# A hybrid encoder layer: rotation tables kept as halves, weight casts issued inside the gates' products, three pairs open at the start of the second SwiGLU

## The chip, the cores and the metric

One core of one Trainium2 chip runs the whole layer. The metric is the device time of one execution in microseconds (us). TensorE multiplies, VectorE (DVE), ScalarE (ACT) and GpSimd (POOL) do the rest; SyncE (SP) and ScalarE issue most of the DMAs.

## The reference

```python
# x: (1, 1024, 1024) float32; D_MODEL 1024, D_FF 2816
h = x + 1/2 * SwiGLU(RMSNorm(x))                  # SwiGLU(x) = (silu(x @ Wg) * (x @ Wu)) @ Wd
z = RMSNorm(h) @ W_in                             # 512 ssm | 512 q | 512 k | 512 v | 1024 gate | 1024 gate
A = GLU(bidirectional S5 of z.ssm) -> 1024        # 32 groups of 16 channels, 64 complex states each
B = 2-D neighbourhood attention of q, k, v -> 1024
h = h + (sigmoid(gate_ssm) * A + sigmoid(gate_att) * B) @ W_out
h = h + 1/2 * SwiGLU(RMSNorm(h))
out = RMSNorm(h)
```

S5 is the linear recurrence s[t] = lambda s[t-1] + B u[t] with complex diagonal lambda, over 1024 positions in both directions, and y[t] = Re(C s[t]).

## The kernel before

**Products.** Everything lies transposed in SBUF, 128 features by two halves of 512 positions. A float32 operand is split in two parts that TensorE takes: hi, a cast by ScalarE, and lo, the rest, a subtraction by VectorE. A product is three: hi x hi, hi x lo, lo x hi. All of them are issued through `mm` (L265), so line 265 stands for nearly all matmuls.

**Weights.** The class `Weights` holds one list of units in the order in which TensorE will need them. A unit "u" is a weight of 128 x 1024 (cast L191, subtraction L192); a unit "p" is one of seven 128 x 512 blocks of a gate and up pair (L176, L202); a unit "h" is a half of a down weight. Raw weights come by SyncE's queue into five buffers `wr` and are issued as buffers come free; split ones lie in eight buffers `wp`. `next(ahead)` prepares units up to `ahead` beyond the current one and hands out the current one. `fill` prepares more while there is room, and may make the cast of the next unit without its subtraction (`cast_one`); `self.cast` and `self.split` count the units whose cast and whose subtraction have been issued. Raw buffers come free when a unit is split, so `drop` and `load` follow it.

**The SwiGLUs.** After some plain blocks in the first layer, a gate and up pair is computed in seven products instead of eight, on sums of blocks (Strassen's way, in Winograd's form): the weights' sums S by VectorE (L134, four a pair, issued by `early` and `step`), the activations' T1 to T4 by VectorE, too. `FIRST` writes out by hand in which order the first pairs' products come: entry "61" is product 6 of the second pair. Before, the first layer has 21 entries with three pairs open at a time, the second 28 with four. Products 1 and 2 need only blocks of the activations themselves; products 6, 7, 5 and 4 need T2, T3, T1 and T4, product 3 the last block scaled. `feed` calls the steps that form the T after given numbers of products; `T` can only be scaled when the normalisation (`rstd`, then a spread product with `diag`) is there. Near the end of a layer, `feed` also loads and splits the first operands of the down projection (`down_load`, `down_split`).

**S5 among the gates.** The state space part is cut in 16 blocks b of two groups. `ssm_steps` is a generator of 21 rounds of seven steps; one step is taken every seven matmuls of the products that run then, so that a round n works on several blocks: enter (block n-4: L265 ps<-su,let, evacuated by ScalarE as ev, L1066 and L1067), rotation (L1079, L1080), leave (block n-5: ps<-sx,lo), scan (L1094) and a second rotation, the shift into sx by ScalarE (L1106, L1107) with the operands of block n-2 (four transposes L1028), the table (block n-3), the powers (L993). The rotation multiplies by a table of cosines and sines over 128 positions: `ssm_table` makes it every fourth round for four blocks, by seven doublings of three instructions each (L1002), each doubling the length by the angle sum rule; the last is made in two parts.

The gates are 16 products of 48 matmuls (`gates`, the units are "u"), whose results ScalarE evacuates and stores (L1229, L1230). With `W.next()`, product c prepares unit c+2 at its start: cast by ScalarE, then subtraction by VectorE, each in its engine's order of issue among the scan's steps.

**Merge and project.** `merge` forms m = sigmoid(gate_ssm) A + sigmoid(gate_att) B for eight blocks d and two halves: x times the first product, y times the second, the sum by GpSimd, and the split of the half before (`ended`). `project` multiplies m by W_out, half 0 first, and adds to h; `done` accumulates the squares for the next normalisation. During half 1, `early(3)` issues three sums of the coming pairs behind d = 4, 5 and 6.

Of the kernel before, what the change touches and what calls it, by code (L numbers as in the profile page):

```python
# [15 lines left out]
P = 128  # L16
KD = 8
# [21 lines left out]
def hs(half):  # L39
# [7 lines left out]
FILLED, ACT, TAIL = 7, 24, 3  # L47
NP = NF // 2

FIRST = (  # L50
    "10 11 12 20 21 22 60 61 70 71 50 51 40 41 62 30 31 72 52 42 32",
    "10 11 12 20 21 22 13 60 61 23 70 71 50 51 40 41 62 30 31 72 52 42 32 63 73 53 43 33",
)
THEN = (1, 6, 2, 7, 5, 4, 3)


def order_of(fs):

    first = [(int(x[1]), int(x[0])) for x in FIRST[len(fs) == NF].split()]
    return [(fs[i], q) for i, q in first] + [(f, q) for f in fs[max(i for i, _ in first) + 1 :] for q in THEN]  # L60


class Weights:
# [85 lines left out]
    def step(self, n=1):  # L149
        for _ in range(min(n, len(self.steps))):  # L150
            self.steps.pop(0)()

    def cast_one(self):

        u = self.units[self.cast]
        if u[0] == "h":
            i = u[1]
            self.load(i + 1)
            src = self.tiles[i][:, :HALF]
        else:  # L160
            p, q = u[1:]
            if q < 3:
                i = self.pairs[p]["raw"]
                self.load(i + 1)
                while i not in self.tiles:
                    self.step()
                    self.load(i + 1)
                src = self.tiles[i][:, hs(q - 1)]
            else:
                self.blocks(p)  # L170
                src = self.pairs[p]["S"][q]
                if q == 6:
                    self.step(5)
        t = self.pool.tile([P, 1024], F32R, tag="wp", name="wp", bufs=PARTS)
        hi, lo = t[:, :HALF], t[:, HALF:]
        self.nc.scalar.copy(hi, src)  # L176
        self.casts[self.cast] = (hi, lo, src)
        self.cast += 1

    def prepare_one(self):  # L180
        nc, u = self.nc, self.units[self.split]
        if u[0] == "u":
            i = u[1]
            self.load(i + 1)
            raw = self.tiles[i]
            n = self.raws[i].shape[1]
            hi, lo = (self.pool.tile([P, 1024], F32R, tag="wp", name="wp", bufs=PARTS) for _ in (0, 1))

            cuts = [0, P, n] if self.split < 2 else [0, n]
            for a, b in zip(cuts, cuts[1:]):  # L190
                nc.scalar.copy(hi[:, a:b], raw[:, a:b])  # L191
                nc.vector.tensor_tensor(  # L192
                    out=lo[:, a:b], in0=raw[:, a:b], in1=hi[:, a:b].bitcast(F32), op=ALU.subtract
                )
            self.parts[self.split] = (hi, lo)
            self.drop(i)
            self.cast += 1
        else:
            if self.cast == self.split:
                self.cast_one()  # L200
            hi, lo, src = self.casts.pop(self.split)
            nc.vector.tensor_tensor(out=lo, in0=src, in1=hi.bitcast(F32), op=ALU.subtract)  # L202
            self.parts[self.split] = (hi, lo)
            if u[0] == "h":
                self.drop(u[1])
            else:
                self.done(*u[1:])
        if self.split in self.jobs:
            self.job(*self.jobs.pop(self.split))
        self.split += 1  # L210
        self.load(len(self.raws))

        if u[0] == "p":
            for v in self.units[self.split : self.split + 4]:
                if v[0] == "p" and v[2] > 2 and self.loaded >= self.pairs[v[1]]["raw"] + 2:
                    self.blocks(v[1])
# [43 lines left out]
class Body:  # L260
# [362 lines left out]
    def feed(self, steps, plain, others={}):  # L623
        rest = {4: ("T3",), 5: ("b12",), 6: ("t1",), 7: ("T1",), 8: ("b22",), 9: ("t4",), 10: ("T4",), 12: ("B22",)}
        last = 7 * (NF - plain) - 1

        def after(n):
            for x in rest.get(n, ()):
                steps[x]()
            if n in others:  # L630
                others[n]()

            if n == last - 5:
                for i in range(2):
                    self.down_load(i)
            if n == last - 1:
                self.down_split(0)

        self.early = ({}, {})
        self.gate_up(plain, after)  # L640
# [357 lines left out]

    def ssm_table(self, b):

        nc, pool, st = self.nc, self.ssm, self.ss[b]
        m = lambda o, x, y, op: nc.vector.tensor_tensor(out=o, in0=x, in1=y, op=op)  # L1002
        if b % 4 == 0:
            tab = self.tab = pool.tile([P, 2, 8, P], F32, tag="tab", name="tab", bufs=1)
            nc.vector.memset(tab[:, 0, :, 0], 1.0)
            nc.vector.memset(tab[:, 1, :, 0], 0.0)
            for i in range(7):
                n = 1 << i

                for a, k in ((0, 8),) if i < 6 else ((0, 4), (4, 4)):  # L1010
                    gs = slice(2 * b + a, 2 * b + a + k)
                    sh = [P, 2, k, n]
                    old, new = tab[:, :, a : a + k, 0:n], tab[:, :, a : a + k, n : 2 * n]
                    y = pool.tile([P, 512], F32, tag="ty", name="ty", bufs=1)[:, : 2 * k * n]
                    y = y.rearrange("p (c g j) -> p c g j", c=2, g=k)
                    m(new, old, self.cosines[:, i, gs].unsqueeze(1).unsqueeze(3).to_broadcast(sh), ALU.mult)
                    m(y, old[:, ::-1], self.sines[:, i, :, gs].unsqueeze(3).to_broadcast(sh), ALU.mult)
                    m(new, new, y, ALU.add)
        st["tab"] = (self.tab, slice(2 * (b % 4), 2 * (b % 4) + 2))

    def ssm_operands(self, b):

# [47 lines left out]
    def rotate(self, x, st):  # L1070

        nc, pool = self.nc, self.ssm
        tab, gs = st["tab"]
        c = tab[:, 0, gs, :].rearrange("p g j -> p (g j)")
        s = tab[:, 1, gs, :].rearrange("p g j -> p (g j)")
        ta = pool.tile([P, 2, 2 * P], F32, tag="ta", name="ta", bufs=1)
        tb = pool.tile([P, 2, 2 * P], F32, tag="tb", name="tb", bufs=1)
        xx = x.rearrange("p c g j -> p c (g j)")
        nc.vector.tensor_tensor(out=ta, in0=xx, in1=c.unsqueeze(1).to_broadcast([P, 2, 2 * P]), op=ALU.mult)  # L1079
        nc.vector.tensor_tensor(out=tb, in0=xx, in1=s.unsqueeze(1).to_broadcast([P, 2, 2 * P]), op=ALU.mult)  # L1080
        return ta, tb
# [138 lines left out]
    def gates(self, u):  # L1220

        nc, W = self.nc, self.W
        for c in range(16):
            w = W.next()
            banks = [self.bank(), self.bank()]
            yield from self.passes(banks, w, lambda i: slice(i * P, i * P + P), *u, range(KD))
            for half in (0, 1):
                g = self.big.tile([P, HALF], F32, tag="b", name="g")
                nc.scalar.copy(g, banks[half])  # L1229
                nc.scalar.dma_start(out=self.gs[c, :, hs(half)], in_=g)  # L1230
# [310 lines left out]
    def merge(self, s, a):  # L1541
# [42 lines left out]
        for d in range(KD):  # L1584
            w = ahead.pop(0) if ahead else W.next()
            pool, tag, n = (self.big, "b", None) if d < 4 else (self.tmp, "act", ACT)
            hi, lo = ([pool.tile([P, HALF], F32R, tag=tag, name="m", bufs=n) for _ in (0, 1)] for _ in (0, 1))
            for half in (0, 1):
                x, y = g.pop((d, 0, half)), g.pop((d, 1, half))
                ps = bs.pop((d, half)) if d < 2 else product(s, w, 0, half)  # L1590
                nc.vector.tensor_tensor(out=x, in0=x, in1=ps, op=ALU.mult)
                ps = product(a, w, 4, half, (3,), ba.pop((d, half))) if d < 2 else product(a, w, 4, half)
                nc.vector.tensor_tensor(out=y, in0=y, in1=ps, op=ALU.mult)
                nc.gpsimd.tensor_tensor(out=x, in0=x, in1=y, op=ALU.add)
                while ended:
                    self.split(*ended.pop(0))
                ended.append((hi[half], lo[half], x))
                if d and ready:
                    scaled(ready[0])
                    sigmoid(ready.pop(0))  # L1600
                if d and (d, half) > (1, 0):
                    load()
            mh.append(hi)
            ml.append(lo)
# [3 lines left out]
    def project(self, m, h, done):  # L1608
        nc, W = self.nc, self.W
        for half in (0, 1):  # L1610
            for d in range(KD):
# [3 lines left out]
                self.poke()  # L1615
                nc.vector.tensor_tensor(out=h[d][half], in0=h[d][half], in1=ps[half], op=ALU.add)
                done(d, half)
                if half and 3 < d < KD - 1:
                    W.early(3)
                if half and d == KD - 2:  # L1620
                    W.fill(PARTS - 2)


    def build(self):
# [303 lines left out]
```

## Time and profile before

| | |
|---|---|
| three runs | 2101.65, 2102.79, 2104.61 us; median 2102.79 |
| the profiled execution | 2104.78 us, its span 2103.0 us |
| TensorE busy (PE) | 2010.0 us, 96% |
| weight loads (PEld) | 1640.2 us, 78% |
| VectorE (DVE) | 1436.6 us, 68% |
| ScalarE (ACT) | 843.9 us, 40% |
| GpSimd (POOL) | 163.5 us, 8% |
| DMA | 315.55 MB, mean 150 GB/s |
| TensorE's granted clock, mean | 0.982 |

The span runs from the first to the last instruction; the shares are of it. The granted clock is a share of 2.4 GHz. PE's busy time contains the time that matmuls take longer at a lower clock. In a row of a timeline, [6.09 <-ACT wp L191] says that the engine was idle for 6.09 us before it, and what released it.

### The profile page before, as it was taken

The numbers are of one execution on the slowest core, as the hardware profiler recorded it, in microseconds if no ns is written. First come the engines' busy times: TensorE is split into PE (matmuls) and PEld (weight loads), VectorE is DVE, ScalarE is ACT, GpSimd is POOL, SyncE is SP. The second block draws the span as 40 slices with busy tenths as digits, with TensorE's granted clock in tenths as the row PEclk, the third lists the DMA queues.
The fourth block names the chain that finished last, engine by engine and source line by source line (L and its number), as shares of the span: only waits on it lengthen the run. The fifth ranks groups of instructions, "written<-read, shape, count | busy, mean of one in ns | idle before, by whom it ended". The sixth has DMA issues, their size and how long they took to land.

```text
span 2103.0 us, 26597 instructions
## 1 busy us (share of the span) xinstructions
PE 2010.0 (96%) x9394; PEld 1640.2 (78%) x9394; DVE 1436.6 (68%) x2655; ACT 843.9 (40%) x1548; POOL 163.5 (8%) x192
## 2 busy tenths in 40 slices
PE   8999999999999998897999999998899999999997
PEld 6878888878888887676877778776688888878886
DVE  6986666658676667856475778667866666657556
ACT  7333223324645233333354573334323332334454
POOL 0001111000000111110000303101001100000000
PEclk9999999999999999998999999999999999999998
DMA  4447666647665332222421333535366565457563
GB/s 182 115 148 178 180 186 175 155 157 271 219 203 192 96 104 81 85 85 82 141 83 49 98 114 132 201 114 129 112 172 181 149 189 155 136 184 270 175 206 117
DMA packets 160358, 315.55 MB, mean 150 GB/s; under 512 B 20352, under 2 KB 31776, under 8 KB 160224
## 3 DMA queue, kind: packets, MB, share of 16 engines
q1 hardware_dynamic: 133920, 274.79, 38.9%
q0 software_dynamic: 15232, 27.59, 8.2%
q10 hardware_dynamic: 11072, 11.47, 1.6%
q8 instruction: 74, 1.21, 0.2%
q14 instruction: 60, 0.49, 0.1%
HBM read 243.83 MB, written 116.10 MB: 171 GB/s over the span
## 4 chain that ended last, share of the span: by engine, by line
PE 68%; DVE 19%; ACT 6%; DMA 3%; issue 2%; ACTq 1%; SPq 0%; POOL 0%; DVEq 0%; POOLq 0%
PE ps L265 67%; DVE wp L192 1%; DVE tab L1002 1%; DVE tq L352 1%; ACT wp L191 1%; DVE gl L1559 1%; DVE wp L202 1%; DMA wr<-in_wu 1%; DVE ta L1079 1%; DVE le L993 1%; DVE ww L1094 1%; DVE lo L993 1%; DVE lt L993 1%; DVE tb L1080 1%; DMA y<-ys 1%
## 5 line engine op out<-in xcount | busy, mean ns | idle before, releaser
L265 PE MATMUL ps<-tq,wp 128*128 128x512 f32 x3444 | 793.2, 392 | 16.5 <-DVE u L576 4.7
L265 PEld LDWEIGHTS ps<-tq,wp 128*128 128x128 f32 x3444 | 651.1, 189 | 157.8 <-ACT t L597 4.4
L265 PE MATMUL ps<-ap,wp 128*128 128x512 f32 (+1 forms) x1884 | 428.9, 389 | 7.4 <-ACT ap L351 4.5
L265 PEld LDWEIGHTS ps<-ap,wp 128*128 128x128 f32 x1884 | 351.6, 190 | 83.2 <-ACT ap L351 5.7
L265 PE MATMUL ps<-uh,wp 128*128 128x512 f32 x1088 | 326.2, 405 | 8.7 <-ACT wp L191 8.7
L265 PEld LDWEIGHTS ps<-uh,wp 128*128 128x128 f32 x1088 | 205.0, 193 | 58.5 <-ACT wp L191 10.1
L202 DVE TENSOR_TENSOR wp<-wr,wp 128x512 fp32r<-128x512 f32 x318 | 217.4, 686 | 34.7 <-ACT wp L176 34.7
L176 ACT CAST wp<-wr 128x512 fp32r<-128x512 f32 x318 | 194.3, 614 | 62.8 <-PE ps L265 49.8
L265 PE MATMUL ps<-ul,wp 128*128 128x512 f32 x544 | 183.8, 400 | 0.7 <-DVE ul L331 0.7
L192 DVE TENSOR_TENSOR wp<-wr,wp 128x1024 fp32r<-128x1024 f32 (+2 forms) x72 | 85.5, 1191 | 121.6 <-ACT wp L191 121.3
L351 ACT CAST ap<-ar 128x512 fp32r<-128x512 f32 x154 | 95.4, 619 | 116.9 <-DMA ar<-tq 106.7
L352 DVE TENSOR_TENSOR ap<-ar,ap 128x512 fp32r<-128x512 f32 x154 | 105.8, 687 | 47.5 <-ACT ap L351 47.3
L265 PEld LDWEIGHTS ps<-ul,wp 128*128 128x128 f32 x544 | 102.9, 192 | 21.8 <-DVE ul L331 1.1
L176 ACT CAST wp<-ws 128x512 fp32r<-128x512 f32 x123 | 75.5, 618 | 101.5 <-PE ps L265 72.3
L606 ACT ACTIVATE v<-v 128x512 f32<-128x512 f32 x41 | 25.9, 632 | 221.9 <-DVE v L576 210.9
L265 PE MATMUL ps<-m,wp 128*128 128x512 f32 x384 | 90.6, 396 | 5.2 <-ACT m L351 3.3
L265 PEld LDWEIGHTS ps<-m,wp 128*128 128x128 f32 x384 | 73.0, 191 | 22.0 <-ACT m L351 3.7
L202 DVE TENSOR_TENSOR wp<-ws,wp 128x512 fp32r<-128x512 f32 x123 | 84.1, 685 | 0.0
L688 DVE SCALAR_TENSOR_TENSOR h<-ps,h 128x512 f32<-128x512 f32 (+1 forms) x76 | 48.6, 657 | 51.6 <-PE ps L265 51.6
L96 POOL DMA_DIRECT2D sums<-in_wd x44 | 37.3, 948 | 590.9 <-DMA sums<-in_wd 590.8
L576 DVE TENSOR_TENSOR v<-t,ps 128x512 f32<-128x512 f32 x41 | 28.1, 686 | 70.8 <-PE ps L265 70.8
L191 ACT CAST wp<-wr 128x1024 fp32r<-128x1024 f32 (+2 forms) x72 | 71.0, 995 | 10.0 <-ACT g L1229 7.2
(208 smaller groups left out, 2184.8 us busy)
## 6 DMA issues: line engine op xcount, KB each, us to landing
ar<-tq SPq DMA_DIRECT2D x154, 256.0 KB
wr<-in_wg SPq DMA_DIRECT2D x44, 512.0 KB
wr<-in_wu SPq DMA_DIRECT2D x44, 512.0 KB
sums<-in_wd SPq DMA_DIRECT2D x88, 256.0 KB
wr<-sums SPq DMA_DIRECT2D x88, 256.0 KB
wr<-in_wd SPq DMA_DIRECT2D x66, 256.0 KB
tq<-t SPq DMA_DIRECT2D x61, 256.0 KB
wr<-in_w_in SPq DMA_DIRECT2D x28, 512.0 KB
```

The lines of the kernel that those rows point to most:

```text
L96: self.nc.gpsimd.dma_start(out=out, in_=x, accum_op=ALU.add, max_dma_last_dim=2048)
L176: self.nc.scalar.copy(hi, src)
L191: nc.scalar.copy(hi[:, a:b], raw[:, a:b])
L192: nc.vector.tensor_tensor(out=lo[:, a:b], in0=raw[:, a:b], in1=hi[:, a:b].bitcast(F32), op=ALU.subtract)
L202: nc.vector.tensor_tensor(out=lo, in0=src, in1=hi.bitcast(F32), op=ALU.subtract)
L265: self.nc.tensor.matmul(out, lhsT, rhs, start=start, stop=stop, skip_group_check=go_on)
L351: self.nc.scalar.copy(hi, x)
L352: self.nc.vector.tensor_tensor(out=lo, in0=x, in1=hi.bitcast(F32), op=ALU.subtract)
L576: add = lambda o, u, v: nc.vector.tensor_tensor(out=o, in0=u, in1=v, op=ALU.add)
L606: nc.scalar.activation(out=s["v"], in_=s["v"], func=AF.Silu, scale=-1.0)
L688: nc.vector.scalar_tensor_tensor(out=t, in0=bank[:, sl], scalar=c, in1=t, op0=ALU.mult, op1=ALU.add)
L993: m = lambda o, x, y, op: self.nc.vector.tensor_tensor(out=o, in0=x, in1=y, op=op)
```

## The change

- **Tables in halves.** The table of four blocks holds 64 positions instead of 128, after six doublings. For each block a tile `own` of 128 positions is filled: two ScalarE copies of the first 64, and one doubling of three VectorE instructions into the last 64. `rotate` reads `own`.
- **Casts in the gates' products.** After matmul 24 of each gates' product, `cast_ahead` issues ScalarE's cast of the next unit, if no unit is cast but not split; `prepare_one` then only subtracts.
- **Second layer's order.** Both layers use the order of 21 entries, with three pairs open.
- **Sums among more projections.** `early(4)` behind d = 3, 4 and 5 in the place of `early(3)` behind 4, 5 and 6, and the `fill` behind d = 6 is gone.
- **Merge and down operands.** The split of the half before is issued ahead of the second product's multiplication; the very last sum is VectorE's. The first operands of the down projection are loaded and the first is split two products earlier.

```diff
-FIRST = ("10 11 12 20 21 22 60 61 70 71 50 51 40 41 62 30 31 72 52 42 32",
-    "10 11 12 20 21 22 13 60 61 23 70 71 50 51 40 41 62 30 31 72 52 42 32 63 73 53 43 33",)
+FIRST = "10 11 12 20 21 22 60 61 70 71 50 51 40 41 62 30 31 72 52 42 32"
...
+    def cast_ahead(self):
+        if self.cast == self.split and self.units[self.cast][0] == "u":
+            i = self.units[self.cast][1]
+            if i < self.loaded:
+                hi, lo = (self.pool.tile([P, 1024], F32R, tag="wp", name="wp", bufs=PARTS) for _ in (0, 1))
+                n = self.raws[i].shape[1]
+                self.nc.scalar.copy(hi[:, :n], self.tiles[i][:, :n])
+                self.casts[self.cast] = (hi, lo)
+                self.cast += 1
...
-            if n == last - 5:
+            if n == last - 7:
                 for i in range(2):
                     self.down_load(i)
-            if n == last - 1:
+            if n == last - 3:
                 self.down_split(0)
...
+        def double(new, old, i, a, k):
+            ...
+            m(new, old, self.cosines[:, i, gs].unsqueeze(1).unsqueeze(3).to_broadcast(sh), ALU.mult)
+            m(y, old[:, ::-1], self.sines[:, i, :, gs].unsqueeze(3).to_broadcast(sh), ALU.mult)
+            m(new, new, y, ALU.add)
...
-            tab = self.tab = pool.tile([P, 2, 8, P], F32, tag="tab", name="tab", bufs=1)
+            tab = self.tab = pool.tile([P, 2, 8, 64], F32, tag="tab", name="tab", bufs=1)
...
-            for i in range(7):
+            for i in range(6):
...
+        own = pool.tile([P, 2, 2, P], F32, tag="own", name="own", bufs=2)
+        old = self.tab[:, :, 2 * (b % 4) : 2 * (b % 4) + 2, :]
+        for c in (0, 1):
+            nc.scalar.copy(own[:, c, :, 0:64], old[:, c])
+        double(own[:, :, :, 64:P], old, 6, 2 * b, 2)
+        st["tab"] = own
...
-            yield from self.passes(banks, w, lambda i: slice(i * P, i * P + P), *u, range(KD))
+            for n, _ in enumerate(self.passes(banks, w, lambda i: slice(i * P, i * P + P), *u, range(KD))):
+                if n == 24:
+                    W.cast_ahead()
+                yield
...
+                while ended:
+                    self.split(*ended.pop(0))
                 ps = product(a, w, 4, half, (3,), ba.pop((d, half))) if d < 2 else product(a, w, 4, half)
                 nc.vector.tensor_tensor(out=y, in0=y, in1=ps, op=ALU.mult)
-                nc.gpsimd.tensor_tensor(out=x, in0=x, in1=y, op=ALU.add)
-                while ended:
-                    self.split(*ended.pop(0))
+                (nc.vector if (d, half) == (KD - 1, 1) else nc.gpsimd).tensor_tensor(out=x, in0=x, in1=y, op=ALU.add)
...
-                if half and 3 < d < KD - 1:
-                    W.early(3)
-                if half and d == KD - 2:
-                    W.fill(PARTS - 2)
+                if half and 2 < d < 6:
+                    W.early(4)
```

## Rows read from the trace of the kernel before

**Rows 1.** Windows: stretch, length, busy PE, PEld, DVE, ACT, POOL; granted clock; DMA share; GB/s.

```profile
740.00:1000.00 260.00, 229.48 (x1172) 191.25 (x1171) 179.68 (x366) 87.43 (x165) 27.73 (x47) 0.94 0.27 86
800.00:820.00 20.00, 16.73 (x81) 14.05 (x81) 19.14 (x40) 4.96 (x10) 3.27 (x6) 0.92 0.29 85
820.00:840.00 20.00, 18.85 (x89) 15.93 (x90) 10.41 (x19) 8.03 (x15) 1.78 (x3) 0.83 0.27 87
880.00:900.00 20.00, 14.59 (x65) 12.32 (x64) 13.60 (x24) 5.05 (x9) 1.78 (x3) 0.83 0.21 68
960.00:980.00 20.00, 8.63 (x37) 7.23 (x36) 13.57 (x27) 5.71 (x10) 1.78 (x3) 0.66 0.19 63
819.80:893.10 73.30, 64.65 (x328) 53.53 (x328) 52.58 (x110) 25.07 (x50) 8.79 (x15) 0.95 0.27 86
1405.00:1515.00 110.00, 94.54 (x383) 74.60 (x382) 90.85 (x151) 45.12 (x77) 6.69 (x8) 0.94 0.44 127
```

**Rows 2.** TensorE's waits, 700 to 1020 us: total, times, longest.

```profile
PE ps L265 <- ACT sx L1107: 26.2, 9, 11.4
```

**Rows 3.** Timeline of VectorE, a plain round: start, length, instruction, idle before.

```profile
835.84 0.76 DVE L1103 TENSOR_TENSOR ta<-ta,tb 128x256 f32<-128x256 f32 x2
...
842.70 1.22 DVE L192 TENSOR_TENSOR wp<-wr,wp 128x1024 fp32r<-128x1024 f32 x1 [6.09 <-ACT wp L191]
...
847.89 0.69 DVE L1079 TENSOR_TENSOR ta<-ev,tab 128x512 f32<-128x512 f32 x1
...
852.62 0.76 DVE L1103 TENSOR_TENSOR ta<-ta,tb 128x256 f32<-128x256 f32 x2
```

**Rows 4.** Timeline of ScalarE, the same round.

```profile
836.63 0.62 ACT L1106 COPY sx<-ta 64x508 f32<-64x508 f32 x1 [9.29 <-DVE ta L1103]
...
841.61 1.05 ACT L191 CAST wp<-wr 128x1024 fp32r<-128x1024 f32 x1 [0.41 <-ACT g L1229]
...
843.15 0.58 ACT L1067 COPY ev<-ps 64x512 f32<-64x512 f32 x1
```

**Rows 5.** Timeline of TensorE, another plain round.

```profile
916.03 0.60 PE L1028 MATMUL ps<-ident,le 128*128 128x128 f32 x4
...
922.46 1.05 PE L265 MATMUL ps<-su,let 128*128 128x128 f32 x8
...
928.05 0.71 PE L265 MATMUL ps<-sx,lo 128*128 128x128 f32 x4 [1.13 <-ACT sx L1107]
...
932.49 0.60 PE L1028 MATMUL ps<-ident,le 128*128 128x128 f32 x4
```

**Rows 6.** Timeline of VectorE, a round that makes a table.

```profile
872.60 0.07 DVE L1005 MEMSET tab<- 128x8 f32 x1
...
875.65 0.42 DVE L1002 TENSOR_TENSOR ty<-tab,sines 128x256 f32<-128x256 f32 x1
...
878.62 0.69 DVE L1002 TENSOR_TENSOR tab<-tab,kept 128x512 f32<-128x512 f32 x1
```

**Rows 7.** Timelines of TensorE and VectorE, opening of the second layer.

```profile
1408.28 16.61 PE L265 MATMUL ps<-m,wp 128*128 128x512 f32 x72 [1.60 <-ACT wp L191]
...
1415.58 0.68 DVE L134 TENSOR_TENSOR ws<-wr 128x512 f32<-128x512 f32 x1
...
1438.56 1.02 PE L265 MATMUL ps<-diag,ones 128*128 128x512 f32 x2
...
1445.83 0.68 DVE L431 TENSOR_TENSOR tf<-tf,ps 128x512 f32<-128x512 f32 x1
```

**Rows 8.** Chain of the work that ended last, same opening: start, length, what.

```profile
1412.97 3.91 DMA wr<-in_wg
...
1437.84 6.10 DMA wr<-in_wu
```

**Rows 9.** Timeline of TensorE, end of the merge.

```profile
1334.79 0.51 PE L265 MATMUL ps<-m,wp 128*128 128x512 f32 x1 [3.25 <-ACT m L351]
```

**Rows 10.** Timeline of TensorE, beginning of the first down projection.

```profile
461.47 0.50 PE L265 MATMUL ps<-ap,wp 128*128 128x512 f32 x1 [2.31 <-ACT ap L351]
```

More of the change, by code (lines that the diff above doesn't have):

```diff
@@ L48 @@
 NP = NF // 2
[L50 to L53, printed above, removed]
+FIRST = "10 11 12 20 21 22 60 61 70 71 50 51 40 41 62 30 31 72 52 42 32"
 THEN = (1, 6, 2, 7, 5, 4, 3)
 def order_of(fs):
-    first = [(int(x[1]), int(x[0])) for x in FIRST[len(fs) == NF].split()]
+    first = [(int(x[1]), int(x[0])) for x in FIRST.split()]
     return [(fs[i], q) for i, q in first] + [(f, q) for f in fs[max(i for i, _ in first) + 1 :] for q in THEN]
@@ L186, in prepare_one @@
             n = self.raws[i].shape[1]
-            hi, lo = (self.pool.tile([P, 1024], F32R, tag="wp", name="wp", bufs=PARTS) for _ in (0, 1))
+            if self.split in self.casts:
+                hi, lo = self.casts.pop(self.split)
+            else:
+                hi, lo = (self.pool.tile([P, 1024], F32R, tag="wp", name="wp", bufs=PARTS) for _ in (0, 1))
             cuts = [0, P, n] if self.split < 2 else [0, n]
             for a, b in zip(cuts, cuts[1:]):
-                nc.scalar.copy(hi[:, a:b], raw[:, a:b])
+                if self.cast == self.split:
+                    nc.scalar.copy(hi[:, a:b], raw[:, a:b])
                 nc.vector.tensor_tensor(
@@ L196, in prepare_one @@
             self.drop(i)
-            self.cast += 1
+            self.cast = self.split + 1
         else:
@@ L1002, in ssm_table @@
         m = lambda o, x, y, op: nc.vector.tensor_tensor(out=o, in0=x, in1=y, op=op)
+        def double(new, old, i, a, k):
+            n = old.shape[-1]
+            gs = slice(a, a + k)
+            sh = [P, 2, k, n]
+            y = pool.tile([P, 512], F32, tag="ty", name="ty", bufs=1)[:, : 2 * k * n]
+            y = y.rearrange("p (c g j) -> p c g j", c=2, g=k)
+            m(new, old, self.cosines[:, i, gs].unsqueeze(1).unsqueeze(3).to_broadcast(sh), ALU.mult)
+            m(y, old[:, ::-1], self.sines[:, i, :, gs].unsqueeze(3).to_broadcast(sh), ALU.mult)
+            m(new, new, y, ALU.add)
         if b % 4 == 0:
-            tab = self.tab = pool.tile([P, 2, 8, P], F32, tag="tab", name="tab", bufs=1)
+            tab = self.tab = pool.tile([P, 2, 8, 64], F32, tag="tab", name="tab", bufs=1)
             nc.vector.memset(tab[:, 0, :, 0], 1.0)
             nc.vector.memset(tab[:, 1, :, 0], 0.0)
-            for i in range(7):
+            for i in range(6):
                 n = 1 << i
[L1010 to L1019, printed above, removed]
+                double(tab[:, :, :, n : 2 * n], tab[:, :, :, 0:n], i, 2 * b, 8)
+        own = pool.tile([P, 2, 2, P], F32, tag="own", name="own", bufs=2)
[4 more added lines that the diff above has]
+        st["tab"] = own
     def ssm_operands(self, b):
@@ L1072, in rotate @@
         nc, pool = self.nc, self.ssm
-        tab, gs = st["tab"]
-        c = tab[:, 0, gs, :].rearrange("p g j -> p (g j)")
-        s = tab[:, 1, gs, :].rearrange("p g j -> p (g j)")
+        tab = st["tab"]
+        c = tab[:, 0].rearrange("p g j -> p (g j)")
+        s = tab[:, 1].rearrange("p g j -> p (g j)")
         ta = pool.tile([P, 2, 2 * P], F32, tag="ta", name="ta", bufs=1)
```

## The prediction

> **What bounds the kernel now.** I read the page first, then the windows, then TensorE's waits by stretch, then one round of the stretch that lost most. TensorE is busy for 96% of the span, so no change can bring more than the few per cent in which it stands or runs at half clock. The windows say where these are: from 740 to 1000 us it is busy for 229.48 of 260 us, 30.5 idle, and in four 20 us windows of that stretch its granted clock is 0.92, 0.83, 0.83 and 0.66 [rows 1]. The clock has two levels, 1.2 and 2.4 GHz, so a busy microsecond at a mean of 0.83 does 0.83 us of work: 16.73 x 0.08 + 18.85 x 0.17 + 14.59 x 0.17 + 8.63 x 0.34 = 9.9 us. The stretch loses 40.4 us in all. The other large loser is 1405 to 1515 us, the opening of the second SwiGLU: 15.5 idle and 94.54 x 0.06 = 5.7 by the clock, 21 us [rows 1].
>
> In the first stretch the gates' projections run and the S5 scan is threaded through them. Almost all of TensorE's idle time there ends with ScalarE's sx [rows 2]. A plain round is a ring of two engines. VectorE ends the scan (L1103, 835.84), then stands 6.09 us until ScalarE has cast the next weight (842.70), splits it, does the powers, rotates (847.89), scans, and ends the next scan: 852.62 - 835.84 = 16.78 us [rows 3]. ScalarE stands 9.29 us for VectorE, copies sx, evacuates, and reaches the cast only at 841.61 [rows 4]. Neither is full; each waits for the other. TensorE has less to do: from one round's transposes to the next 932.49 - 916.03 = 16.46 us, of which 1.13 is the wait for sx, so 15.33 us of work [rows 5].
>
> **The early cast.** It is the edit that counts. The cast of a later weight moves from the end of a product to its middle, after 24 of 48 matmuls. In ScalarE's queue it then stands behind ev and ahead of sx of the same round, inside the 9.29 us in which ScalarE does nothing [rows 4]. Its buffers are those of the product before, which TensorE has ended, and its raw weight was issued several products earlier, so it adds no wait. VectorE goes from L1103 straight on. Its next possible wait is ev: from sx to the end of ev it was 843.73 - 836.63 = 7.1 us, less the cast's 0.95, plus half a microsecond for the new copies, 6.7 us; then rotation and scan, 853.4 - 847.9 = 5.5. That ring is 12.2 us, under TensorE's 15.33, so TensorE sets the pace.
>
> **Tables in halves.** Of a table the memsets and six doublings stay: 878.62 - 872.60 = 6.0 us [rows 6]. The seventh goes: six instructions of 0.69, 4.1 us. Each of the four blocks gets three instructions of 256 elements at 0.42 [rows 6], 1.26 us a round, and two ScalarE copies a quarter the size of ev's, which take 1.2 the pair [rows 4]: 0.5, at most 1.2. VectorE does 0.9 us more in four rounds, but no longer ten in a piece. Is there room? Four rounds took 73.30 us, with VectorE busy 52.58 and some 2 in gaps between its own instructions (a plain round's own work is 16.78 - 6.09 = 10.69) [rows 1, 3]. With the halves that is 55.5; TensorE needs 4 x 15.33 and half a microsecond for a small product, 61.8.
>
> The lag of a table round is covered too. After its enter (922.46) TensorE asks for sx of the round before at 926.92, 4.5 us on [rows 5], so sx of this round is due 15.33 + 4.5 = 19.8 us after this enter. The scan ends 7.6 us after it (0.9 enter, 1.2 ev, 5.5). In a table round VectorE then waits for the small product, about 1.5 us behind the transposes, which come 10.0 after enter: 11.5. Then 0.3, the table's 6.0, 1.26, split and powers 5.2, the next scan 5.5 and sx 1.3: 31.1. It is due at 15.33 + 19.8 = 35.1. Four microseconds are spare, and each plain round behind it gives 3 more. So I count all stalls of the stretch as gone, and with them the low clock, which the windows show only where TensorE had waited.
>
> An instruction of 256 elements takes 0.42 us and one of 512 takes 0.69, so half the width does not take half the time [rows 6]. The Trainium skill, "VectorE: DVE Perf Modes", section "The TRN2 errata", speaks against this edit: instructions on SBUF pay a fixed latency each, and it advises tiles of at least 512 elements. The trace agrees on the price, 12 x 0.42 - 6 x 0.69 = 0.9 us per four rounds. By the rule, were VectorE the pace, four tables would give back 3.6 us and the time would be 2068; by the rows it is not the pace, and I cost it at nothing.
>
> Sum of the stretch: 40.4 by windows. By rounds: 73.3 - 61.8 = 11.5 for four, 2.9 for each of the 13 between the first table and the last long wait, 37. I take 38. Bounds 30 and 40.4.
>
> **The merge.** TensorE waits 3.25 us for m at its end [rows 9]. That is the cast of the half before the last, which in ScalarE's queue still stands behind the same sigmoid, which waits for VectorE's scaling. Splitting before the second product moves one VectorE instruction of 0.6. The last sum on VectorE instead of GpSimd concerns a half that the projection reads eight products later. I take 0; bounds -0.6 and +0.6.
>
> **The second layer's opening.** Three effects. (a) The fourth pair's first product needed a raw weight issued at 1437.84 that took 6.10 us; ScalarE's cast waited for it, and VectorE behind the cast, so that the scaling of T began at 1445.83 [rows 7, 8]. The seventh product of the new order reads sums formed long before, so VectorE can scale T when the spread product is there, 1438.56 + 1.02 = 1439.6: 6.2 us won on the engine that is dense from there on. (b) Two products that need no T are gone from ahead of it, so each set of operands is due 24 x 16.61 / 72 = 5.5 us sooner [rows 7]; 5.5 lost. Three pairs fit the banks, so waits for a bank turn into waits for T4 and for evacuations. (c) The first pair's four sums now stand ahead of the split that frees a buffer for the second pair's gate weight. A sum's row shows 0.68 us; neighbours overlap, so I count 0.6 each, 2.4 in all. That weight's issue moves from 1412.97 to 1415.4, and it lands 3.91 us later, or 6.10, the two transfers that the chain shows [rows 8], at 1419.3 or 1421.5. VectorE reaches the sums that read it 2.4 after 1415.6 [rows 7], at 1418.0, and stands 1.3 to 3.5 us. Three sums, 1.8 us, leave the place between the last two projections; there VectorE waits for products anyway, so little of it comes back. Counted to the last row sum, on which the normalisation waits, I take 1.1 us lost, 3.2 at worst. Together -6.2 + 5.5 + 1.1 = +0.4, which I take as 0. Bounds -6 and +8.7, and up to 5 more by the clock.
>
> **Down projections.** The first operand is split two products earlier: about 0.2 us of waiting goes in each layer. The large wait there, 2.31 us [rows 10], is for an operand that is still issued behind the first product. -0.5 in all; bounds -1 and +0.5.
>
> **Sum.** The profiled execution took 2104.8 us, 1.8 of it outside the span of 2103.0. 2104.8 - 38 - 0.5 = 2066.3. It lies 2.0 over the median of the runs, 2102.8, so I forecast **2064**.
>
> **Rivals.**
> (A) The copies become the new wait. ScalarE writes one half of own and VectorE the other. If they are ordered by tile and not by region, VectorE stands in every round until ScalarE is through sx, two evacuations and the copies, some 3.5 of the 4.98 us from sx to the cast [rows 4]. VectorE's plain round is then 10.69 + 1.26 + 3.5 = 15.4, TensorE's pace with nothing left for the tables, so four rounds take about 61.8 + 6. Gain 37 - 13 x 1.5 = 18: 2084. For it: sx stands ahead of the copies. Against: no such wait between two writers of one buffer is in the waits, though no row excludes it either. 11%.
> (B) VectorE, full to 90%, still comes late in the table rounds. Of waits of up to 11.4 us [rows 2] some 2.5 stay in each of four, 10 us with the clock. 2074. 8%.
> (C) The early cast does nothing, as it is made only where two counters agree: the ring of 16.78 stays, the copies put 0.5 ahead of the cast in each round, the shorter table gives 4 back in four. 2103. 2%.
> (D) Slower: the opening of the second layer. Place: the first products on T1 and T4, with VectorE dense (90.85 of 110 [rows 1]). Price: 8.7 and 5 by the clock, 14. It decides only if the gates bring less than 14: with 7 there, 2110; with nothing, 2117. 5%, as the ring would have to hold too.
>
> **How the numbers follow.** Forecast 74%, with a range of its own of 2058 to 2071 (gates 33 to 40.4, opening -3 to +3). The range, 2056 to 2086, takes in B, A and most of the opening's -6. A measurement of this kernel tells about 0.2%, 4 us, from no change. Faster 74 + 11 + 8 = 93%, within 0.2% 2%, slower 5%.
>
> **What would show it.** Right: in the gates' stretch TensorE waits for sx no more than 1 us in sum, its clock reads 1.00, a round takes 15.3 to 15.6 us, and the cast lies ahead of sx. VectorE waiting for own's copies would mean A; waits for sx behind the four tables alone, B; VectorE still waiting 6 us for the cast, C. In the opening no wait of 10 us of ScalarE for a weight, and a new wait of TensorE of 4 to 6 us ahead of T4's first product; if it runs through there, my 5.5 was too high. I am wrong as a whole if the gates' stretch is not at least 30 us shorter.

## The result, and the profile after

The changed kernel takes 2064.35 us (median of four runs, 2062.95 to 2069.7) against 2103.39 (four runs): a ratio of 0.9814, with a 95% interval of 0.98 to 0.9828. The profiled execution took 2063.81 us, its span 2062.0, 41.0 us less than before; between the two medians it is 39.0. The forecast of 2064 was met, but that it was met so closely is luck: its sum held two misses that nearly cancel.

Landmarks on TensorE cut both executions at the same work: the first table product (ps<-cs,flat), the first product of the values (ps<-wp,uh), the first and the last of the projection (ps<-m,wp), and the first and the last of the second layer's down projection (ps<-ap,wp). Each length below is the difference of two starts or ends in the timeline.

| stretch, us | before | after | difference | in the forecast |
|---|---|---|---|---|
| up to the table product (first layer, four projections) | 701.05 | 700.01 | -1.0 | -0.5 for the two down projections together |
| gates with the scan | 292.67 | 249.87 | -42.8 | -38 |
| values, attention, first part of the merge | 334.48 | 334.44 | 0 | 0 |
| projection, with the wait for the merge's end | 96.69 | 102.41 | +5.7 | 0 |
| second SwiGLU with its opening | 442.77 | 441.90 | -0.9 | 0 |
| its down projection | 223.66 | 221.17 | -2.5 | in the -0.5 above |

The gates first. The windows of the changed kernel, columns as in [rows 1]: the first is the stretch of [rows 1], the second holds the same 1331 matmuls that before took 262.28 us of TensorE's busy time in a stretch of 292.80.

```profile
740.00:1000.00 260.00, 260.00 (x1369) 218.85 (x1369) 198.46 (x412) 110.35 (x215) 32.40 (x51) 1.00 0.33 109
700.00:950.00 250.00, 250.00 (x1331) 209.78 (x1330) 209.47 (x442) 102.98 (x213) 34.94 (x59) 1.00 0.34 108
```

TensorE never stands there, and its clock stays at 2.4 GHz. VectorE's timeline shows the rounds behind a table, to be held against [rows 3]:

```profile
852.81 0.42 DVE L1015 TENSOR_TENSOR own<-tab,kept 128x256 f32<-128x256 f32 x1
...
863.86 0.76 DVE L1123 TENSOR_TENSOR ta<-ta,tb 128x256 f32<-128x256 f32 x2
864.54 1.22 DVE L204 TENSOR_TENSOR wp<-wr,wp 128x1024 fp32r<-128x1024 f32 x1
...
871.25 0.69 DVE L1099 TENSOR_TENSOR ta<-ev,own 128x512 f32<-128x512 f32 x1 [0.50 <-ACT ev L1087]
...
875.98 0.76 DVE L1123 TENSOR_TENSOR ta<-ta,tb 128x256 f32<-128x256 f32 x2
...
898.49 0.69 DVE L1099 TENSOR_TENSOR ta<-ev,own 128x512 f32<-128x512 f32 x1 [3.42 <-ACT ev L1087]
```

The subtraction (L204) now follows the end of the scan at once. From one end of a scan to the next, 863.86 to 875.98, it is 12.1 us, against 16.78 before; after two such rounds VectorE has caught up and waits 3.42 us for ev, that is, for TensorE. ScalarE, to be held against [rows 4], makes the cast (L157) behind ev and 5.5 us ahead of sx:

```profile
882.83 0.58 ACT L1087 COPY ev<-ps 64x512 f32<-64x512 f32 x1
883.44 1.05 ACT L157 CAST wp<-wr 128x1024 fp32r<-128x1024 f32 x1
...
888.98 0.62 ACT L1126 COPY sx<-ta 64x508 f32<-64x508 f32 x1 [1.83 <-DVE ta L1123]
```

TensorE's pace is the distance of two enters, 15.02 us:

```profile
866.13 1.05 PE L277 MATMUL ps<-su,let 128*128 128x128 f32 x8
...
881.15 1.05 PE L277 MATMUL ps<-su,let 128*128 128x128 f32 x8
```

The merge is the loss. TensorE's waits of the changed kernel from 1280 to 1460 us (total, times, longest): the first row answers to [rows 9], the last lies between the projection's halves and is 1.60 us as before [rows 7], the others belong to the second layer's opening.

```profile
PE ps L277 <- ACT m L363: 8.7, 1, 8.7
PE ps L277 <- ACT tq L363: 5.4, 1, 5.4
PE ps L277 <- DVE acc L296: 3.8, 1, 3.8
PE ps L277 <- DVE u L588: 2.9, 1, 2.9
PE ps L277 <- ACT wp L203: 1.6, 1, 1.6
```

And the opening on TensorE and VectorE, answering to [rows 7]: VectorE waits for the spread product (3.02 us) and scales T 1.06 us after that product's start, where it was 7.27 before; T4's first product then waits 5.37 us.

```profile
1403.21 1.02 PE L277 MATMUL ps<-diag,ones 128*128 128x512 f32 x2
...
1404.27 0.69 DVE L443 TENSOR_TENSOR tf<-tf,ps 128x512 f32<-128x512 f32 x1 [3.02 <-PE ps L277]
...
1438.85 3.65 PE L277 MATMUL ps<-tq,wp 128*128 128x512 f32 x7 [5.37 <-ACT tq L363]
```

### The profile page after: what moved, and what is told of

It is laid out like the page before. It is cut to its first block, busy times and chain, and to the rows that moved or that the text cites. A ratio compares the mean times of both kernels' runs of the same rounds, so it can differ in the third digit from the quotient of the medians.

```text
span 2062.0 us, 26647 instructions
## 1 busy us (share of the span) xinstructions
PE 1994.0 (97%) x9394; PEld 1629.6 (79%) x9394; DVE 1435.7 (70%) x2680; ACT 852.5 (41%) x1580; POOL 162.0 (8%) x191
## 4 chain that ended last, share of the span: by engine, by line
PE 83%; DVE 9%; ACT 3%; DMA 3%; issue 1%; SPq 0%; POOL 0%; ACTq 0%; DVEq 0%
PE ps L277 82%; DMA y<-ys 1%; DVE tq L364 1%; DVE wp L214 1%; PE ps L1369 1%; DMA h<-in_x 1%; DVE wp L204 1%; DMA wr<-in_wg 1%; DVE ws L131 0%; DMA ar<-tq 0%; ACT sq L294 0%; DVE h L432 0%; PE ps L1048 0%; DVE tf L443 0%; DVE gl L1582 0%
## 5 line engine op out<-in xcount | busy, mean ns | idle before, releaser
L204 DVE TENSOR_TENSOR wp<-wr,wp 128x1024 fp32r<-128x1024 f32 (+2 forms) x72 | 84.6, 1179 | 52.1 <-ACT wp L203 51.9
L609 ACT COPY t<-ps 128x512 f32<-128x512 f32 x41 | 24.0, 586 | 112.9 <-PE ps L277 112.9
```

Of the source, the lines that this page charges most:

```text
L204: nc.vector.tensor_tensor(out=lo[:, a:b], in0=raw[:, a:b], in1=hi[:, a:b].bitcast(F32), op=ALU.subtract)
L609: nc.scalar.copy(s["t"], ps)
```

## The experiments

Two groups of four, each group on one chip. The ratios are to runs of the kernel before on the same chip. The lengths are those of the landmarks, from one profiled execution each: gates / projection with the wait for the merge's end / second SwiGLU / its down projection. Of old merge this execution is the shortest of its four (2054.49 us, the median is 2060.06), of old opening the longest of its five (2070.91, the median is 2067.83).

| kernel | gates | projection | second SwiGLU | down | time, ratio to before |
|---|---|---|---|---|---|
| before | 292.67 | 96.69 | 442.77 | 223.66 | |
| after | 249.87 | 102.41 | 441.90 | 221.17 | 0.9814 (0.98 to 0.9828) |
| cast alone | 251.29 | 96.68 | 443.41 | 222.75 | 0.9804 (0.979 to 0.9818) |
| halves alone | 291.71 | 96.71 | 442.78 | 223.48 | 1.0001 (0.9992 to 1.001) |
| old merge | 249.87 | 96.72 | 439.79 | 220.64 | 0.9775 (0.9759 to 0.9792) |
| old opening | 249.87 | 102.57 | 442.96 | 224.30 | 0.9817 (0.9804 to 0.983) |
| last sum only | 249.88 | 98.37 | 439.73 | 224.47 | 2061.98 us, one run |
| cast in the merge | 249.87 | 90.20 | 441.72 | 221.03 | 0.9741 (0.9728 to 0.9754) |
| old sums | 249.87 | 102.66 | 439.15 | 222.25 | 2061.99 us, one run |
| cast at 44 | 261.79 | 102.66 | 441.91 | 221.65 | 2076.76 us, one run |

**1. Cast alone.** The kernel before, with the changed kernel's `cast_ahead`, its call in `gates` and its `prepare_one`, and nothing else.

```diff
+    def cast_ahead(self):
+        ...
-            yield from self.passes(banks, w, lambda i: slice(i * P, i * P + P), *u, range(KD))
+            for n, _ in enumerate(self.passes(banks, w, lambda i: slice(i * P, i * P + P), *u, range(KD))):
+                if n == 24:
+                    W.cast_ahead()
+                yield
```

> The kernel before with the early cast alone; the table of 128 positions stays. Theory R (the ring of the two engines through the weight's cast is the cause, and the cast alone breaks it): from the first ps<-cs,flat to the first ps<-wp,uh, 292.7 us before and 249.9 after the whole change, it takes 250 to 252; TensorE waits for sx under 2 us in sum; the time is 2061 to 2063, as VectorE's table of ten microseconds in one piece still fits. Rival H (the burst of the table is the cause): the waits at and behind the four tables stay, 25.1 of the 30.5 us, with the clock that they cost; only the plain rounds' 5.4 go, and the time is about 2097.

It took 2065.45 us against 2105.77, and the gates 251.29. The gates came as expected; the time lies 2.5 us over the 2061 to 2063 expected. One wait for sx is left, in the first round that has such a product; in the waits of TensorE from 700 to 950 us it is the only row:

```profile
PE ps L280 <- ACT sx L1122: 1.1, 1, 1.1
```

So the ring through the cast was the cause; the table in one piece of ten microseconds costs no more than this wait once the ring is open. The ratio of the cast alone, 0.9804, can't be told from that of the whole change, 0.9814: together, the other four edits gain nothing that these times show.

**2. Halves alone.** The kernel before, with the changed kernel's `ssm_table` and `rotate`.

```diff
-        st["tab"] = (self.tab, slice(2 * (b % 4), 2 * (b % 4) + 2))
+        for c in (0, 1):
+            nc.scalar.copy(own[:, c, :, 0:64], old[:, c])
+        double(own[:, :, :, 64:P], old, 6, 2 * b, 2)
+        st["tab"] = own
```

> The kernel before with the tables in halves alone; the cast stays where it was. Theory R: VectorE still stands about 6 us in a plain round for the cast, the two copies put 0.5 us more ahead of it in each round, the shorter table gives back 4 us in four: 2095 to 2107, I take 2100. Rival H: the waits behind the tables go, 25 us and the clock's 12: 2066 to 2070.

2106.12 us: no change, at the upper end of what was expected. VectorE's waits from 740 to 960 us, in this kernel first and in the one before second: nearly all of them are still ahead of the subtraction that follows the cast (L192). The profile puts one of these waits down to TensorE.

```profile
DVE wp L192 <- ACT wp L191: 53.4, 11, 6.1
DVE wp L192 <- PE ps L1036: 5.9, 1, 5.9
```

```profile
DVE wp L192 <- ACT wp L191: 57.8, 10, 6.9
```

The plain round is longer, 17.74 us from one end of a scan to the next (835.63 to 853.37) against 16.78, by the copies and the three instructions of `own`; what the shorter table gives is spent there. Rival H fell twice.

**3. Old merge.**

```diff
-                while ended:
-                    self.split(*ended.pop(0))
                 ps = product(a, w, 4, half, (3,), ba.pop((d, half))) if d < 2 else product(a, w, 4, half)
                 nc.vector.tensor_tensor(out=y, in0=y, in1=ps, op=ALU.mult)
-                (nc.vector if (d, half) == (KD - 1, 1) else nc.gpsimd).tensor_tensor(out=x, in0=x, in1=y, op=ALU.add)
+                nc.gpsimd.tensor_tensor(out=x, in0=x, in1=y, op=ALU.add)
+                while ended:
+                    self.split(*ended.pop(0))
```

> The changed kernel with the merge as it was before: the split of the half before behind the sum, the last sum on GpSimd. Theory M (VectorE and ScalarE are the merge's pace, 11.25 us a block before against TensorE's 10.9, and the moved split makes it 11.83): the wait of 8.69 us for m at the merge's end falls to 3.0 to 3.5, the time to 2058 to 2059.5. Rival F (the gates' faster stretch feeds the merge later, by its queues): the wait stays over 7 us, the time stays at 2064.

2060.06 us, 0.6 over what was expected, and the wait for m is 3.2 us again, the projection's stretch 96.72. By this stretch, the merge's part of the change costs 5.7 us.

**4. Old opening.** The 28 entries and the old sums are back.

```diff
-    first = [(int(x[1]), int(x[0])) for x in FIRST.split()]
+    first = [(int(x[1]), int(x[0])) for x in FIRST[len(fs) == NF].split()]
...
-                if half and 2 < d < 6:
-                    W.early(4)
+                if half and 3 < d < KD - 1:
+                    W.early(3)
+                if half and d == KD - 2:
+                    W.fill(PARTS - 2)
```

> The changed kernel with the second layer's old order of 28 entries, its sums among three projections and the fill behind the seventh. My sum of the three effects: as long to within 1.5 us, the stretch from the last ps<-m,wp to the first ps<-ap,wp of the layer 443 us against 442.06: 2064 to 2066. Rival G (the 6.2 us that VectorE no longer stands are a gain, and the lost 5.5 were covered): 2069 to 2071. Rival L (the earlier T4 costs more than the early weight brings): under 2061.

2067.83 us, between the 2064 to 2066 expected and rival G's 2069; a ratio of 0.9817, which can't be told from the changed kernel's 0.9814. The stretch took 442.96, as expected. All four executions with the old order lie between 442.77 and 443.41, the five with the new order and the new sums between 439.73 and 441.91, so the new opening wins some 2 us (0.9 to 3.7), where 0.4 lost was forecast. TensorE's idle time in the stretch says the same: 13.9 to 15.4 us in the four, 12.2 to 13.7 in the five. The new order's own spread is not one of its large waits (3.8, 2.9 and 5.3 to 5.5 us in each); it goes with the granted clock. The first 100 us of the stretch, in the changed kernel (441.90) and in experiment 3 (439.79):

```profile
1386.73:1486.73 100.00, 87.52 (x350) 70.24 (x351) 80.45 (x137) 40.60 (x73) 6.69 (x8) 0.91 0.43 124
1380.02:1480.02 100.00, 86.30 (x359) 69.06 (x360) 82.34 (x141) 40.60 (x73) 6.68 (x8) 0.95 0.43 124
```

The clock there is 0.91 in the three longer stretches of the new order and 0.95 in the two shorter ones. Why it differs is open.

**5. Last sum only.** The split is back behind the sum; the last sum stays VectorE's.

```diff
-                while ended:
-                    self.split(*ended.pop(0))
                 ps = product(a, w, 4, half, (3,), ba.pop((d, half))) if d < 2 else product(a, w, 4, half)
                 ...
+                while ended:
+                    self.split(*ended.pop(0))
                 ended.append((hi[half], lo[half], x))
```

> The changed kernel with the split of the half before put back behind the sum; the very last sum stays VectorE's. Theory M (the moved split alone lengthens VectorE's ring in each block of the merge): the wait for m at the merge's end is 3.2 to 3.5 us as before the change, and the stretch from the first to the last ps<-m,wp takes 96.5 to 97 us against 102.41. Rival P (the last sum on VectorE, in line with the other work, makes the wait): the wait stays over 8 us, the stretch at 102.

The wait was 3.24 us, as with the old merge: the moved split alone makes the long wait, and rival P fell. But the stretch took 98.37 us, 1.4 more than expected. Against the old merge's 96.72, from which only the last sum differs, 0.5 of the 1.65 us is the next wait, for m's subtraction, 0.8 us where it is 0.3 there:

```profile
PE ps L277 <- DVE m L364: 0.8, 1, 0.8
```

The other 1.1 us are busy time (92.69 against 91.56) at a clock of 0.97 against 0.98. So of the 5.7 us the moved split makes 4.0; the rest comes with the last sum on VectorE, and one execution does not show how much of it would come again.

**6. Cast in the merge.** On top of experiment 3:

```diff
                 ended.append((hi[half], lo[half], x))
+                if d and half:
+                    W.cast_ahead()
...
                 self.poke()
+                W.cast_ahead()
                 nc.vector.tensor_tensor(out=h[d][half], in0=h[d][half], in1=ps[half], op=ALU.add)
```

> The changed kernel with the merge's old order, and the early cast used there and in the projection too: in the merge behind the split in the second half of each block from the second on, in the projection ahead of the sum with h. Theory M: VectorE's 1.64 us a block for the next weight's cast go, its pace in the merge is then about 9.6 us against TensorE's 10.9, and the wait for m at the end, 3.25 us, falls under 0.5; in the projection the 1.6 us for a weight between its halves goes. The stretch from the first to the last ps<-m,wp takes 91.5 to 93 us, and the time is 4 to 5 us below that of the old order in the merge alone (0.9775 of before): 0.9755. Rival S (the end waits for the chain from the last product through the scaling, sigmoid and sum, whatever VectorE's pace): 3.2 us stay, 0.977.

2051.49 us (five runs, 2050.18 to 2052.0), faster than both kernels: 0.9741. VectorE's timeline: near the merge's end it now waits for TensorE, as in neither kernel there, and its subtraction (L204) waits for nothing:

```profile
1266.82 1.21 DVE L204 TENSOR_TENSOR wp<-wr,wp 128x1024 fp32r<-128x1024 f32 x1
1267.96 0.67 DVE L1614 TENSOR_TENSOR gl<-gl,ps 128x512 f32<-128x512 f32 x1
...
1274.19 0.69 DVE L1616 TENSOR_TENSOR gl<-gl,ps 128x512 f32<-128x512 f32 x1 [1.06 <-PE ps L277]
```

TensorE goes from the merge into the projection without a wait, and the 1.6 us for a weight between the projection's halves are gone too; a wait of 0.85 us for a weight's subtraction near the projection's end is the only one left. 90.20 is even below the 91.5 expected: TensorE's busy time fell as well, from the old merge's 91.56 to 89.34 us, with the clock at 1.00 where it was 0.98. Rival S fell: the merge's end waited for nothing but VectorE's lag.

**7. Old sums.** The order of 21 entries stays, the sums stand where they stood before.

```diff
-                if half and 2 < d < 6:
-                    W.early(4)
+                if half and 3 < d < KD - 1:
+                    W.early(3)
+                if half and d == KD - 2:
+                    W.fill(PARTS - 2)
```

> The changed kernel with the sums of the coming pairs behind projections 4, 5 and 6, three each, and the fill, as before; the order of 21 entries stays. By my third effect, the wait for the last row sum falls from 3.84 to 2.9 us, and the stretch from the last ps<-m,wp to the first ps<-ap,wp is about 1 us shorter, 440.9. Rival: the sums then stand between the last projections and the first products and are late there: no shorter, or up to 2 us longer.

The wait for the last row sum is 3.1 us, not 3.8: the third effect is there, at 0.7 us. The stretch took 439.15, 2.8 less than in the changed kernel where 1 was expected; 2.1 of that is busy time (427.31 against 429.42), and the five kernels of experiment 4 with the new order differ by more (426.05 to 429.74).

**8. Cast at 44.**

```diff
-                if n == 24:
+                if n == 44:
                     W.cast_ahead()
```

> The changed kernel with the early cast at matmul 44 of a gates' product in the place of 24, so that in ScalarE's queue it stands behind sx in most rounds, but still ahead of the evacuations. Theory R (its place ahead of sx is what opens the ring): VectorE waits for the cast again, 3 to 4.5 us a round, its plain round is near TensorE's 15.3, and the table rounds are late: 260 to 275 us from the first ps<-cs,flat to the first ps<-wp,uh, about 2079 in all. Rival O (it is enough that the cast is issued within the product before): 249.9 as with 24, 2064.

261.79 us and 2076.76: theory R, at its lower end. VectorE's waits from 740 to 960 us in this kernel, and in the changed one behind it (there the row of 6.7 us is at 958.00, after the gates):

```profile
DVE wp L204 <- ACT wp L157: 27.5, 9, 4.1
DVE ta L1099 <- ACT ev L1087: 10.8, 4, 4.4
```

```profile
DVE ta L1099 <- ACT ev L1087: 21.5, 11, 7.3
DVE wp L204 <- ACT wp L203: 6.7, 1, 6.7
DVE k0o L981 <- PE ps L277: 3.7, 2, 3.1
```

Behind sx, the cast makes VectorE wait again, and the slack is not enough behind the tables: TensorE stands 7.4 us for sx, in four waits, the longest 2.4. The other 4.5 us are busy time, 254.38 us for the same 1331 matmuls against 249.87; some 3 of them lie in three windows with a lower clock:

```profile
870.00:880.00 10.00, 8.00 (x41) 6.68 (x40) 5.81 (x13) 3.75 (x7) 0.00 (x0) 0.87 0.02 5
880.00:890.00 10.00, 10.00 (x53) 8.21 (x52) 9.71 (x20) 2.36 (x6) 1.78 (x3) 0.95 0.46 144
940.00:950.00 10.00, 8.29 (x39) 6.92 (x40) 5.58 (x14) 6.21 (x12) 1.78 (x3) 0.83 0.45 145
```

## Why the prediction was right, and where it was not

**The ring and its opening: right, shown.** The cast alone gives 41.4 of the 42.8 us, the halves alone 1.0, and the place of the cast decides (12 us between matmul 24 and 44). The forecast ring of 12.2 us measured 12.1. In the table round the path from enter to the end of sx was put at 31.1 us and due at 35.1; it went from 835.60 to 865.9, 30.3, and the product that reads it came at 870.43, 34.8 behind that enter. Four microseconds spare were forecast, 4.5 were there.

**The size of the gates' gain: 38 forecast, 42.8 measured, outside the bound of 40.4.** The step that failed is the clock: "a busy microsecond at a mean of 0.83 does 0.83 us of work", 9.9 us in all (the terms add up to 10.0). The same 1331 matmuls were busy for 262.28 us before and 250.00 after, 12.3. A window's mean clock covers idle time as well as busy time. With the busy time alone it gives 10.0, with the whole windows 20 x (0.08 + 0.17 + 0.17 + 0.34) = 15.2; the truth lay between, which fits a low clock that fell on the busy part more than evenly. And I took 38, between the 40.4 by windows and the 37 by rounds. The rounds were low by TensorE's need, "4 x 15.33 and half a microsecond", 61.8 us: without waits four rounds take 60.60 (enters at 835.60 and 896.20), a plain one 15.02 and not 15.3 to 15.6, and (73.30 - 60.60) / 4 x 13 is 41.3.

**Halves: the cost of nothing was right.** The rule from "VectorE: DVE Perf Modes" (the Trainium skill, section "The TRN2 errata") is true of the price, 0.42 us for 256 elements in the changed kernel, as before, against 0.69 for 512: half the width takes more than half the time. From start to start the difference is smaller, 0.7 us in four rounds and not 0.9: the three of `own` take 1.14 us (852.81 to 853.95), the six of the seventh doubling took 3.87 (878.62 to 882.49). But VectorE was not the pace. Nor was there much to win: with the old table and the cast the gates take 251.29. The edit is worth 1.4 us here, most of it the one wait of 1.1.

**The merge: wrong.** The failed step is "Splitting before the second product moves one VectorE instruction of 0.6 ... I take 0". It was costed once, at the end, and TensorE's waits show only the end. The rows to read were VectorE's round in the merge, here of the kernel before:

```profile
1318.16 0.68 DVE L1591 TENSOR_TENSOR gl<-gl,ps 128x512 f32<-128x512 f32 x1
...
1328.27 1.22 DVE L192 TENSOR_TENSOR wp<-wr,wp 128x1024 fp32r<-128x1024 f32 x1 [1.64 <-ACT wp L191]
1329.41 0.68 DVE L1591 TENSOR_TENSOR gl<-gl,ps 128x512 f32<-128x512 f32 x1
```

A block took it 11.25 us, of which 1.64 was the wait for the next weight's cast behind the sigmoids; TensorE needs 10.88 (half a block from one ps<-sp,wp to the next, 1317.32 to 1322.76). VectorE was already the pace, by 0.4 a block, and the wait of 3.25 us at the end was its lag, as experiment 6 showed. The moved split makes VectorE stand for m's cast, and in the changed kernel a block takes 11.83 (1271.30 to 1283.13):

```profile
1271.30 0.68 DVE L1614 TENSOR_TENSOR gl<-gl,ps 128x512 f32<-128x512 f32 x1
1272.59 0.69 DVE L364 TENSOR_TENSOR m<-gl,m 128x512 fp32r<-128x512 f32 x1 [0.61 <-ACT m L363]
...
1277.89 1.22 DVE L204 TENSOR_TENSOR wp<-wr,wp 128x1024 fp32r<-128x1024 f32 x1 [1.70 <-ACT wp L203]
...
1283.13 0.68 DVE L1614 TENSOR_TENSOR gl<-gl,ps 128x512 f32<-128x512 f32 x1
```

That is 0.58 a block, over seven blocks 4.1 of the 5.4 us by which the wait grew; the rest I have not taken apart. Experiment 5 finds the moved split behind the whole 5.4. Experiment 6 turns the same reading into a gain: 1.64 a block less, and the lag never forms.

**The opening: near, by its parts.** (a) 6.2 us won was forecast for the start of the scaling, and 7.27 - 1.06 = 6.2 came. (b) A new wait of 4 to 6 us ahead of T4's first product was forecast, and 5.37 came. (c) 1.1 us lost at the row sum was forecast; it was 1.0 (3.84 against 2.88), 0.7 by experiment 7. VectorE stood for the late weight as forecast (1.3 to 3.5 us), by 1.49 us, where the kernel before has no such wait:

```profile
1381.14 0.69 DVE L131 TENSOR_TENSOR ws<-wr 128x512 f32<-128x512 f32 x1 [1.49 <-DMA wr<-in_wg]
```

Their sum was a little off: some 2 us won instead of 0.4 lost. How (a) and (b) share that was not tried apart.

**Down projections: nothing.** The wait of 2.31 us became 2.05, in the second layer 2.25 became 2.23. The 2.5 us that the second layer's down projection took less can't be put down to the change: in the seven kernels with its new code the stretch lies between 220.64 and 224.47 us, and the three with the old code (222.75 to 223.66) lie inside that. In the execution before, its first windows showed a granted clock of 0.96 and 0.95, in the one after 1.00.

**The rivals.** A: VectorE never waited for the copies of `own` (its waits of the gates' stretch stand under experiment 8: ev, and the small product ahead of a table). B and C: no wait for sx behind a table, and the cast lies ahead of sx. D did not come: the opening was not longer. What it feared there happened in the merge, a stage in which VectorE was the pace and was made slower.

## What to carry to other kernels

When two engines hand work to each other in a loop, follow the loop once round, from the one to the other and back, and hold its length against the pace of the engine that should be the bound. Neither engine has to be full for the loop to be too long: VectorE's own work was 10.69 of 16.78 us. What one of them waits for counts with everything that stands ahead of it in the other's queue, so an instruction's place there can matter more than its cost: a cast of 1.05 us, moved ahead of sx, took 4.7 us off the round. Do this for every loop in which an edit falls, not only for the one with the large waits: a wait that is seen once, at the end of a stage, can be a lag that grew a little in each round. And when a forecast is met, set its terms against the stretches: here a loss of 5.7 us that was costed at nothing hid 4.8 us more in the gates than forecast, and 2.5 that are not the change's.

## What the runs showed that was not expected

Waits of one length can cost different amounts behind them. In experiment 8, TensorE waited 2.37 us before 813.33 and its clock stayed at 2.4 GHz in the windows behind; after 2.00 us before 876.21 and 2.45 before 941.71 it fell, as the three windows show. In the opening, the same large waits went with stretches that differ by 2.2 us from one execution to another, and with clocks of 0.91 and 0.95 in their first 100 us. Differences under some 3 us in one stretch are therefore read here from its waits and its busy time, not from its length alone.
